# One ring of split weights, weight sums by accumulating transfers, and one more pair by seven in the second half's down projection

## The chip, the cores and the metric

The kernel runs on one core of a Trainium2 chip. The metric is device time in microseconds of one execution. Three executions of the kernel before took 1452.99 to 1454.95 us, median 1453.46 us.

## The reference

One encoder layer for 256 tokens of width 2048, all in float32. The matrix products are nearly all of the work:

- `proj = rms_norm(x) @ w_in`, 10240 columns: queries, keys and values of two attentions (windowed with grouped queries, and dilated in three patterns), and two gates of 2048 columns each;
- `merged = sigmoid(ga) * (ya @ w_branch_a) + sigmoid(gb) * (yb @ w_branch_b)`, then `x + merged @ w_out`;
- `x + (gelu(conv3(hf @ w_ffn_gate)) * (hf @ w_ffn_up)) @ w_ffn_down` with 5632 hidden columns;
- `x + sigmoid(rms_norm(x) @ w_ple_gate) * (p @ w_ple_proj)`, and a last rms norm.

## The kernel before

**Split numbers.** Every operand of a large product is split into a high and a low half in a fast 32-bit format: ScalarE (ACT) copies the high half (L310), VectorE (DVE) subtracts it from the original for the low half (L311). A product is then three matmuls (`thirds`, L413 to L415: high by high, high by low, low by high), or, where the weights are the stationary operand, one of 512 columns and one of 256 (L356, L363).

**Pieces and units.** The weights lie in DRAM as 258 pieces of 128 rows by 2048 columns (1 MB), in the order in which they are used. SyncE's queue (SP) loads a piece into one of three buffers `raw` (`load`, L251), two pieces ahead of the one being split. A piece is split in units (`produce`, L293), each `uh` or `vh` (high) and `ul` or `vl` (low). Units sit in two rings: "u" with six slots and "v" with two, each slot 1024 columns wide whatever the unit's width. `pump` (L318) splits further units whenever a slot is given back (`drop`, L330), strictly in the list's order.

**Stages.** In order of time: A (38 projection jobs, with the attention between them), four gate stages B0 to B3, each followed by the two branch products `ba` and `bb`, two halves of the output projection D0 and D1, then the MLP in two halves of 22 hidden chunks: E0 (gate and up, 44 jobs of 16 matmul pairs), F00 and F01 (down, half of the output columns each), E1, F10 and F11. At the end stand the `ple` stages pp0, pp1, G0, G2, G3.

**Seven products for eight.** B, D, F and G0 work on a pair of 128-row weight chunks by two blocks of 512 output columns at a time, a 2 x 2 x 2 block product for two halves of the tokens. A piece marked "s" does its eight products plainly. One marked "Z" or "S" does seven (M1 to M7) with sums of weight blocks and sums of activations, and adds the results at the end of the stage. A string has a letter for each piece; the second half's down projection, for instance, is "ZsZsZsZsZss", five of eleven by seven, in each of F10 and F11. Each M has a bank of the accumulator memory: M1 to M7 in seven banks, P22 in the eighth; the plain pieces use M2, M3, M4 and P22. The last piece of each string is plain. While it runs, `row_sums` (L910) adds M1, M6, M7 and M5 into the result tiles (L917 to L921), and then each of M2, M3, M4 and P22 is added when its last product is done (in D and F by `finish` of `residual`, L1033 and L1035). A seven-product piece has four units; M1 needs the first, M2 and M3 the second, M7 and M6 (M5 in an "S") the third, the other two the fourth. They run in the order M1, M7, M6 or M5, M5 or M6, M4, M2, M3, and give their units back in the order first, third, fourth, second.

**Sums of weights.** The sums of the four blocks in `raw` are made by DVE: L283 and L284 for Z (512 and 1024 columns), L289 to L291 for S (1024, 512 and 512). One sum of three blocks of a Z piece is made ahead: `sum_ahead` (L263) loads half of the three blocks into SBUF by GpSimd's queue (POOL, L269), DVE adds them (L272, L273), and POOL stores the result to DRAM (L276), from where `load` takes it in place of the first block. In A this is done for the Z pieces of B1 to D1 (tile `hb`), in E0 and E1 for those of F and G0 (tile `ahead`), at slots given by job and step (`at` and `run_due`, L596 to L605).

**Order.** The program gives an order and a priority; a planner may put instructions of one engine otherwise where their operands come late in its own estimate, save those under `keep`. On each engine the instructions then run in that fixed order, and each waits for what it needs.

## Time and profile before

| | us |
|---|---|
| median of three runs | 1453.46 |
| the profiled execution | 1453.29 |
| its span (first to last instruction) | 1451.5 |
| PE busy | 1439.8 |
| DVE busy | 1255.9 |
| ACT busy | 836.3 |
| POOL busy | 126.7 |

What lies between an execution's time and its span is the start and the end of the program. "PE" is TensorE's matmuls and "PEld" its weight loads, which overlap them. In a row of instructions stand the start, the duration, the engine, the line, the operation, the tiles written and read, their shapes and the count; in square brackets the idle time before it, and what ended it. Groups give their count, busy time and mean duration in ns, then the idle time before them. The DMA rows give the queue, the count, the size and the median time from issue to landing.

### The profile page before, as it was taken

What the parts mean: (1) busy time and instruction counts of PE and PEld (TensorE: products, weight loads), DVE (VectorE), ACT (ScalarE), POOL (GpSimd) and SP (SyncE); (2) the same over time, 40 slices, a digit from 0 to 9 for tenths busy, and PEclk for the clock granted to TensorE, in tenths of its full rate; (3) what the DMA queues carried; (4) which work ended last, traced back from release to release, by engine and by line L of the source; (5) the groups of instructions that cost most, each with busy time, mean ns of one, the idle gap of its engine ahead of it and who ended that gap; (6) DMA issues with size and microseconds to landing.
All of it is one profiled execution on the core that took longest, in us unless ns stands there. A gap on an engine that the chain in (4) does not pass through costs nothing.

```text
span 1451.5 us, 20060 instructions
## 1 busy us (share of the span) xinstructions
PE 1439.8 (99%) x7455; PEld 1231.0 (85%) x7455; DVE 1255.9 (87%) x1827; ACT 836.3 (58%) x1160; POOL 126.7 (9%) x193
## 2 busy tenths in 40 slices
PE   9999999999999999999999999999999999999997
PEld 8888888888888888788888888888888888888885
DVE  8778776779999999989787899997878799898994
ACT  7455544546656656666555566565545466564863
POOL 0112222210000000000222000000222200000000
PEclk9999999999999999999999999999999999999999
DMA  9776677764456466475777655566777765556462
GB/s 334 274 286 240 227 259 261 255 223 174 177 207 227 172 228 235 170 262 216 272 253 256 240 208 189 198 251 220 256 278 254 276 239 200 198 187 243 163 232 87
DMA packets 67805, 331.17 MB, mean 228 GB/s; under 512 B 8628, under 2 KB 13620, under 8 KB 41340
## 3 DMA queue, kind: packets, MB, share of 16 engines
q1 hardware_dynamic: 52268, 280.46, 53.7%
q0 software_dynamic: 14720, 48.25, 9.2%
q8 instruction: 58, 0.95, 0.3%
q10 hardware_dynamic: 720, 1.19, 0.2%
q14 instruction: 39, 0.32, 0.1%
HBM read 315.67 MB, written 14.20 MB: 227 GB/s over the span
## 4 chain that ended last, share of the span: by engine, by line
PE 92%; DVE 3%; issue 2%; DMA 1%; ACT 0%; POOL 0%; POOLq 0%; SPq 0%; DVEq 0%; ACTq 0%
PE bank L356 28%; PE bank L363 15%; PE bank L413 13%; PE bank L414 13%; PE bank L415 13%; PE bank L340 2%; PE bank L402 1%; PE bank L404 1%; PE bank L403 1%; PE bank L341 1%; DVE ul L311 1%; PE bank L966 1%; DMA raw<-in_wts 1%; DVE vl L311 1%; DMA xr<-in_xrow 0%
## 5 line engine op out<-in xcount | busy, mean ns | idle before, releaser
L310 ACT ACTIVATE uh<-raw 128x1024 fp32r<-128x1024 f32 (+2 forms) x519 | 515.4, 1007 | 293.1 <-PE bank L415 88.8
L311 DVE TENSOR_TENSOR ul<-raw,uh 128x1024 fp32r<-128x1024 f32 (+2 forms) x519 | 590.7, 1157 | 63.5 <-ACT uh L310 42.6
L356 PE MATMUL bank<-hf,uh 128*128 128x512 f32 x1408 | 336.6, 391 | 0.0
L356 PEld LDWEIGHTS bank<-hf,uh 128*128 128x128 f32 x1408 | 258.8, 188 | 50.6 <-DVE hf L522 0.4
L363 PEld LDWEIGHTS bank<-hf,ul 128*128 128x128 f32 x1408 | 180.7, 191 | 7.0
L363 PE MATMUL bank<-hf,ul 128*128 128x256 f32 x1408 | 183.3, 283 | 0.0
L310 ACT ACTIVATE vh<-raw 128x1024 fp32r<-128x1024 f32 x106 | 111.0, 1055 | 56.1 <-DVE raw L283 29.9
L311 DVE TENSOR_TENSOR vl<-raw,vh 128x1024 fp32r<-128x1024 f32 x106 | 127.3, 1217 | 1.7 <-ACT vh L310 0.5
L356 PE MATMUL bank<-hs,uh 128*128 128x512 f32 x432 | 103.6, 392 | 0.0
L356 PEld LDWEIGHTS bank<-hs,uh 128*128 128x128 f32 x432 | 79.5, 188 | 15.6
L414 PE MATMUL bank<-ul,act 128*128 128x512 f32 x218 | 84.8, 389 | 0.0
L415 PE MATMUL bank<-uh,act 128*128 128x512 f32 x218 | 84.8, 389 | 0.0
L413 PE MATMUL bank<-uh,act 128*128 128x512 f32 x218 | 84.5, 389 | 0.0
L505 ACT ACTIVATE t<-bank 128x256 f32<-128x256 f32 x122 | 45.4, 375 | 60.8 <-PE bank L363 50.1
L269 POOL DMA_DIRECT2D ahead<-in_wts x52 | 38.8, 747 | 378.5 <-DMA ahead<-ahead 209.3
L1112 ACT ACTIVATE gw<-gw,cl 128x256 f32<-128x256 f32 x44 | 24.1, 594 | 71.5 <-DVE gw L1109 71.4
L413 PE MATMUL bank<-uh,hs 128*128 128x512 f32 x154 | 60.8, 395 | 0.0
L272 DVE TENSOR_TENSOR ahead<-ahead 128x256 f32<-128x256 f32 x52 | 21.9, 422 | 44.7 <-DMA ahead<-in_wts 44.6
L415 PE MATMUL bank<-uh,hs 128*128 128x512 f32 x154 | 60.1, 390 | 0.0
L414 PE MATMUL bank<-ul,hs 128*128 128x512 f32 x154 | 60.0, 389 | 0.0
L363 PE MATMUL bank<-hs,ul 128*128 128x256 f32 x432 | 56.6, 284 | 0.0
L284 DVE TENSOR_TENSOR raw<-raw 128x1024 f32<-128x1024 f32 x46 | 56.0, 1217 | 0.3
(270 smaller groups left out, 2526.1 us busy)
## 6 DMA issues: line engine op xcount, KB each, us to landing
raw<-in_wts SPq DMA_DIRECT2D x205, 1024.0 KB, 4.9
raw<-in_wts SPq DMA_DIRECT2D x46, 768.0 KB, 4.6
ahead<-in_wts POOLq DMA_DIRECT2D x52, 384.0 KB, 5.1
hb<-in_wts POOLq DMA_DIRECT2D x40, 384.0 KB, 5.0
raw<-ahead SPq DMA_DIRECT2D x46, 256.0 KB, 4.9
ahead<-ahead POOLq DMA_DIRECT2D x52, 128.0 KB, 4.5
raw<-in_wts SPq DMA_DIRECT2D x12, 512.0 KB, 6.7
ahead<-hb POOLq DMA_DIRECT2D x40, 128.0 KB, 3.1
```

Source lines behind the costliest of these rows:

```text
L269: keep(nc.gpsimd.dma_start(q, wts[p][:, :3 * WIDE].rearrange("p (q c) -> p q c", c=WIDE)[:, :, cols]))
L284: nc.vector.tensor_tensor(raw[:, 2 * WIDE:], raw[:, 2 * WIDE:], view(q[0], 0, (0, 2), (1, WIDE)), op=ALU.subtract)
L310: nc.scalar.activation(hi, src, AF.Copy)
L311: nc.vector.tensor_tensor(lo, src, hi.bitcast(F32), op=ALU.subtract)
L340: nc.tensor.matmul(acc, hi[:, w], m, start=first, stop=False, skip_group_check=True)
L356: nc.tensor.matmul(acc, weights(u)[0][:, o * P:(o + 1) * P], m, start=first, stop=False, skip_group_check=True)
L363: nc.tensor.matmul(acc[:, T:], weights(u)[1][:, o * P:(o + 1) * P], m[:, :T], start=False, stop=last, skip_group_check=True)
L413: nc.tensor.matmul(acc, sh, wh, start=first, stop=False)
L414: nc.tensor.matmul(acc, sh, wl, start=False, stop=False)
L415: nc.tensor.matmul(acc, sl, wh, start=False, stop=last)
L505: keep(nc.scalar.activation(t, acc[:, T:], AF.Copy, scale=scale))
L1112: nc.scalar.activation(c[:, i], g[:, i], AF.Identity, scale=tap(1, f), bias=tap(3, f))
```

## The change

- All split weights share one store: 48 blocks of 128 columns from the start, and 16 more when the attention's memory is given back (in B0). A unit takes as many blocks as it is wide, from the front of a list of free blocks (`take`), and gives them back at its end. Where its blocks aren't neighbours, it is split in two parts, each with its own copy and subtraction.
- The seven products run in the units' order: M1, M2, M3, M7, M6, M5, M4. Signs in the sums change to fit (`sums_of`, `row_sums`, `sums_of_weights`).
- The "S" pieces are gone. Their seven places are "Z" now, so their sums are made ahead too. B0 has two of them.
- `sum_ahead` is three transfers on POOL's queue from DRAM to DRAM, a copy and two that accumulate; DVE takes no part. `spread_sums` puts the three steps of each piece two slots apart and the pieces evenly over the slots: those of B0 to B3 over the jobs of A after the eighth, those of D0 and D1 over the pieces of B1 to B3, those of F and G0 over the jobs of E0 and E1 from the thirteenth on.
- The second half's down projection has six of eleven pieces by seven in place of five, in F10 and in F11.

```diff
-GATES = ("sssssSSs", "ZsZZsSZs", "ZsZSsSZs", "ZsZSsSZs")
+GATES = ("sssssZZs", "ZsZZsZZs", "ZsZZsZZs", "ZsZZsZZs")
-DOWN = ("ZZsZsZsZsZs", "ZsZsZsZsZss")
+DOWN = ("ZZsZsZsZsZs", "ZsZZsZsZsZs")
...
-RINGS = {"u": 6, "v": 2}
+STORE = {"w": 48, "v": 16}
...
+    def take(u, n):
+        taken[u] = [free.popleft() for _ in range(n)]
+        runs = []
+        for o, (which, b) in enumerate(taken[u]):
+            if runs and runs[-1][0] == which and runs[-1][1] + runs[-1][3] == b:
+                runs[-1][3] += 1
+            else:
+                runs.append([which, b, o, 1])
+        return runs
...
-    def sum_ahead(p, h, tag):
...
-        keep(nc.gpsimd.dma_start(q, wts[p][:, :3 * WIDE].rearrange("p (q c) -> p q c", c=WIDE)[:, :, cols]))
-        def add():
-            keep(nc.vector.tensor_tensor(q[:, 0], q[:, 2], q[:, 0], op=ALU.subtract))
-            keep(nc.vector.tensor_tensor(q[:, 0], q[:, 0], q[:, 1], op=ALU.add))
-        def store():
-            keep(nc.gpsimd.dma_start(ahead[p][:, cols], q[:, 0]))
+    def sum_ahead(p):
+        ahead[p] = dram.tile([P, WIDE], F32, name="ahead%d" % p)
+        def step(n):
+            keep(nc.gpsimd.dma_start(ahead[p], wts[p][:, n * WIDE:(n + 1) * WIDE], accum_op=ALU.add if n else ALU.bypass))
+        return [partial(step, n) for n in range(3)]
...
     def sums_of_weights(raw):
-        nc.vector.tensor_tensor(q[1], q[0], q[1], op=ALU.subtract)
-        nc.vector.tensor_tensor(raw[:, 2 * WIDE:], raw[:, 2 * WIDE:], view(q[0], 0, (0, 2), (1, WIDE)), op=ALU.subtract)
+        nc.vector.tensor_tensor(raw[:, WIDE:3 * WIDE], view(q[0], 0, (0, 2), (1, WIDE)), raw[:, WIDE:3 * WIDE], op=ALU.subtract)
+        nc.vector.tensor_tensor(q[3], q[0], q[3], op=ALU.add)
...
+        made[u] = take(u, (b - a) // P)
+        for _, _, o, n in made[u]:
+            hi, lo = part_of(made[u], o, n)
+            src = raw[:, a + o * P:a + (o + n) * P]
+            nc.scalar.activation(hi, src, AF.Copy)
+            nc.vector.tensor_tensor(lo, src, hi.bitcast(F32), op=ALU.subtract)
...
-                    todo = (("M1", m1, 0, 0, 0), ("M7", sums[2], 2, 1, None), ("M6", sums[1], 2, 0, 2),
-                            ("M5", sums[0], 3, 0, None), ("M4", m4, 3, 1, 3),
-                            ("M2", m2, 1, 1, None), ("M3", sums[3], 1, 0, 1))
+                todo = (("M1", m1, 0, 0, 0), ("M2", m2, 1, 1, None), ("M3", sums[3], 1, 0, 1),
+                        ("M7", sums[2], 2, 1, None), ("M6", sums[1], 2, 0, 2),
+                        ("M5", sums[0], 3, 0, None), ("M4", m4, 3, 1, 3))
...
+    def spread_sums(pieces, slots):
+        last = len(slots) - 5
+        for e, p in enumerate(pieces):
+            first = e * last // max(len(pieces) - 1, 1)
+            for n, step in enumerate(sum_ahead(p)):
+                at(slots[first + 2 * n], step)
...
+    slots = [(i, k) for i in range(FIRST + 1, NA)
+             for k in (range(0, KC, KC // len(_JOBS[i][1])) if _JOBS[i][0] == "v" else (0,))]
+    spread_sums(summed("B0", "B1", "B2", "B3"), slots[:-3])
+    spread_sums(summed("D0", "D1"), [("B%d" % j, i, 0) for j in range(1, 4) for i in range(8)])
...
+        spread_sums(summed("F10", "F11", "G0") if half else summed("F00", "F01"),
+                    [(stage, i, 0) for i in range(12, len(jobs) - joint)])
```

More of the change, by code (lines that the diff above doesn't have):

```diff
@@ L1 @@
 import math
+from collections import deque
 from contextlib import ExitStack
+from functools import partial
 import numpy as np
@@ L247, in _encoder, with extend, part_of @@
     raws, made = {}, {}
-    state = {"raw": 0, "unit": 0, "at": 0, "early": True,
-             "u": RINGS["u"], "v": RINGS["v"]}
+    state = {"raw": 0, "unit": 0, "at": 0, "early": True}
+    store, free, taken = {}, deque(), {}
+    def extend(which, pool):
+        store[which] = [pool.tile([P, STORE[which] * P], FR, name=which + half) for half in ("h", "l")]
+        free.extend((which, b) for b in range(STORE[which]))
+    extend("w", wpool)
+    def take(u, n):
[7 more added lines that the diff above has]
+        return runs
+    def part_of(runs, o, n):
+        which, b, first, size = next(r for r in runs if r[2] <= o < r[2] + r[3])
+        assert o + n <= first + size
+        a = (b + o - first) * P
+        return [t[:, a:a + n * P] for t in store[which]]
     def load(r, a=0, b=PIECE):
@@ L337, in block @@
         u, o = _FBLOCKS[state["at"]]
-        hi, lo = weights(u)
-        w = slice(o * P, (o + 1) * P)
-        nc.tensor.matmul(acc, hi[:, w], m, start=first, stop=False, skip_group_check=True)
-        nc.tensor.matmul(acc[:, T:], lo[:, w], m[:, :T], start=False, stop=last, skip_group_check=True)
+        hi, lo = weights(u, o)
+        nc.tensor.matmul(acc, hi, m, start=first, stop=False, skip_group_check=True)
+        nc.tensor.matmul(acc[:, T:], lo, m[:, :T], start=False, stop=last, skip_group_check=True)
         state["at"] += 1
@@ L442, in cut @@
         def cut(u, i):
-            return [w[:, i * WIDE:(i + 1) * WIDE] for w in weights(u)]
+            return weights(u, 4 * i, 4)
         for i, p in enumerate(pieces):
@@ L683, in _encoder @@
     nc.sync.dma_start(hold, rows)
-    hb = big.tile([P, 2 * D * 2], F32, name="hb", tag="R1")
-    spare = [view(hb, QH * AW + BH * BW + e * 3 * T, (T, 3), (1, T)) for e in range(2)]
+    hb = big.tile([P, QH * AW + BH * BW], F32, name="hb", tag="R1")
     hba = hb[:, :QH * AW].rearrange("p (h c) -> p h c", c=AW)
@@ L857, in after, with summed @@
             attend(i, [(QH + g * HG + j, KVH + g * HG + j) for g in range(NG)], QH + j)
-    todo = [(p, h) for stage in ("B1", "B2", "B3", "D0", "D1") for p in _STAGES[stage] if _PIECES[p][0] == "Z"
-            for h in range(2)]
-    slots = [(FIRST, SUB)]
-    for i in range(FIRST + 1, NA + 2):
-        slots += [(i, k) for k in (range(0, KC, 16 // len(_JOBS[i][1])) if i < NA and _JOBS[i][0] == "v" else (0,))]
-    assert len(todo) < len(slots), (len(todo), len(slots))
-    def asked(e):
-        add, store = sum_ahead(*todo[e], spare[e % 2])
-        i, k = slots[e + 1]
-        late = k + (2 if i < NA and _JOBS[i][0] == "v" else SUB)
-        at((i, late), add)
-        at((i, late + 1), store)
-    for e in range(len(todo)):
-        at(slots[e], asked, e)
+    def summed(*stages):
+        return [p for stage in stages for p in _STAGES[stage] if _PIECES[p][0] == "Z"]
+    slots = [(i, k) for i in range(FIRST + 1, NA)
+             for k in (range(0, KC, KC // len(_JOBS[i][1])) if _JOBS[i][0] == "v" else (0,))]
+    spread_sums(summed("B0", "B1", "B2", "B3"), slots[:-3])
+    spread_sums(summed("D0", "D1"), [("B%d" % j, i, 0) for j in range(1, 4) for i in range(8)])
     for i, job in enumerate(_JOBS):
@@ L904, in open_tok @@
         held["tok"] = ctx.enter_context(tc.tile_pool(name="tok", bufs=1))
+        extend("v", held["tok"])
     def outputs():
@@ L1162, in split_last @@
             nc.vector.tensor_tensor(pl_[k], held["pr"][:, k], ph_[k].bitcast(F32), op=ALU.subtract)
-    def sevens(half):
-        stages = ["F%d%d" % (half, j) for j in range(2)] + ["G0"] * half
-        return [p for stage in stages for p in _STAGES[stage] if _PIECES[p][0] == "Z"]
     for half in range(2):
@@ L1178, in _encoder @@
         turns["e"] = 0
-        todo = [(p, h) for p in sevens(half) for h in range(2)]
+        spread_sums(summed("F10", "F11", "G0") if half else summed("F00", "F01"),
+                    [(stage, i, 0) for i in range(12, len(jobs) - joint)])
         for i, (kind, n) in enumerate(jobs[joint:]):
-            if i > 1 and todo and (i % 2 == 0 or i < LASTS):
-                held["job"] = todo.pop(0), ("act2", "S4")[i % 2]
-                one_ahead(stage)
-            finish_ahead(stage)
+            run_due(stage, i, 0)
             mlp(kind, n, product(stage, lambda k: hf[:, k, :], KC, "e"))
-        assert not todo
-        drain_ahead()
         if half:
```

86 lines of the change are left out of this document (15 added, 71 removed).

## The prediction

> **What bounds the kernel now.** I read the first part of the page, then the stages in the view that cuts the span into stretches (us, then busy time and instructions of PE, PEld, DVE, ACT, POOL, then granted clock, DMA share, GB/s). The stretches shown are the projections of A, the last gate stage B3, the output stage's second half D1, the second MLP half E1, and its down stages F10 and F11.
>
> ```profile
> span 1451.5 us, 20060 instructions
> PE 1439.8 (99%) x7455; PEld 1231.0 (85%) x7455; DVE 1255.9 (87%) x1827; ACT 836.3 (58%) x1160; POOL 126.7 (9%) x193
> ...
> 4.40:304.30 299.90, 299.55 (x1723) 262.79 (x1722) 231.81 (x397) 166.37 (x264) 53.52 (x80) 1.00 0.76 270
> 482.30:523.60 41.30, 41.30 (x186) 33.72 (x185) 41.30 (x51) 25.81 (x30) 0.00 (x0) 1.00 0.60 221
> 581.80:624.80 43.00, 42.67 (x193) 34.11 (x192) 42.90 (x54) 27.30 (x36) 0.00 (x0) 1.00 0.53 189
> 984.20:1229.00 244.80, 244.80 (x1409) 216.34 (x1408) 204.93 (x332) 137.71 (x201) 37.01 (x56) 1.00 0.69 247
> 1229.00:1285.50 56.50, 56.50 (x252) 46.83 (x251) 51.34 (x58) 31.43 (x36) 0.00 (x0) 1.00 0.55 205
> 1285.50:1343.00 57.50, 57.50 (x259) 47.50 (x258) 51.17 (x59) 33.84 (x41) 0.00 (x0) 1.00 0.59 217
> ```
>
> TensorE is busy in every stretch at a granted clock of 1.00. VectorE fills B3 and D1 as fully (41.30 of 41.30, 42.90 of 43.00), so there both engines just keep pace. A busy PE need not run at its peak, so I looked at start times. The timeline of PE, start and duration of each matmul, in F10:
>
> ```profile
> 1249.77 0.39 PE L414 MATMUL bank<-ul,act 128*128 128x512 f32 x1
> ...
> 1255.89 0.39 PE L414 MATMUL bank<-ul,act 128*128 128x512 f32 x1
> ```
>
> Between these two stand 26 others, so 27 steps take 6.12 us: **0.227 us for each matmul of 512 columns**, whatever its listed duration. Time lost is what a stage takes beyond that step. The same view has the first matmul of D1, its neighbours and the first one after it:
>
> ```profile
> 581.21 0.39 PE L413 MATMUL bank<-uh,merged 128*128 128x512 f32 x1
> ...
> 582.58 0.50 PE L413 MATMUL bank<-vh,S 128*128 128x512 f32 x1 [0.30 <-DVE c L919]
> ...
> 583.84 0.39 PE L413 MATMUL bank<-uh,merged 128*128 128x512 f32 x1
> ...
> 584.75 0.39 PE L413 MATMUL bank<-vh,S 128*128 128x512 f32 x1
> ...
> 624.74 1.52 PE L356 MATMUL bank<-hf,uh 128*128 128x512 f32 x6
> L966 PE MATMUL bank<-ident,xr 128*128 128x128 f32 x64 | 9.8, 273 | 0.0
> ```
>
> D1 has five pieces by seven and three by eight: (5 x 7 + 3 x 8) x 3 = 177 matmuls, 40.2 us, and 16 transposes at 9.8/64 = 0.15 us, 2.4 us. It took 43.5 us, so some **0.95 us is lost**, half of it in the second product, whose bank DVE's L919 emptied late. One more loss, from A, where the five matmuls ought to end at 111.77 + 5 x 0.227 = 112.91:
>
> ```profile
> 111.77 1.29 PE L356 MATMUL bank<-hs,uh 128*128 128x512 f32 x5
> 113.41 0.39 PE L711 MATMUL bank<-near,v 128*128 128x256 f32 x1 [0.35 <-DVE near L770]
> 108.93 0.42 DVE L272 TENSOR_TENSOR hb<-hb 128x256 f32<-128x256 f32 x1 [0.51 <-DMA hb<-in_wts]
> ```
>
> Attention waits 0.50 us for L770. Shortly before, DVE stood 0.51 us at an addition for a sum ahead until its load came, with everything behind it in its queue.
>
> **The change part by part.** (1) *One more pair by seven in F10 and in F11.* Each drops one of eight products: 2 x 3 matmuls x 0.227 = **-1.36 us**, on the bound engine. In exchange DVE makes 3584 columns of low halves for that piece where it made 2048, and sums over 1536:
>
> ```profile
> L311 DVE TENSOR_TENSOR vl<-raw,vh 128x1024 fp32r<-128x1024 f32 x106 | 127.3, 1217 | 1.7 <-ACT vh L310 0.5
> L284 DVE TENSOR_TENSOR raw<-raw 128x1024 f32<-128x1024 f32 x46 | 56.0, 1217 | 0.3
> L272 DVE TENSOR_TENSOR ahead<-ahead 128x256 f32<-128x256 f32 x52 | 21.9, 422 | 44.7 <-DMA ahead<-in_wts 44.6
> L291 DVE TENSOR_TENSOR raw<-raw 128x512 f32<-128x512 f32 x7 | 4.8, 681 | 0.0
> ```
>
> That is 1.22 + 0.68 of low halves and 1.22 + 0.68 of sums, 3.8 us a stage: F10 goes to 55.1 of 55.8 us, F11 to 55.0 of 56.8. B3 shows that DVE can be full without holding PE. ACT's share of it (about 1.7 us) lies inside F10's 31.43 of 56.5. The new pair's own sums of activations, about 1.5 us of DVE, fall into E1 (204.93 of 244.80). Without that cover it would be PE's wait.
>
> (2) *Sums ahead by transfers alone.* Two additions of this form (L272, L273) go for each half piece, 52 times in the E stages and 40 times in A: 2 x 0.42 x 92 = 77 us of DVE off a path that DVE doesn't set, in A and the two E stages. What PE gets of it is the wait in A: bound 0 to -0.50 us, and since the transfers that DVE waited for are no longer DVE's, I take **-0.50**. In exchange POOL issues 55 x 3 = 165 transfers of 256 KB, one copy and two accumulates a piece, where it issued 184 before. No accumulate stands in the trace. Behind a POOL wait only more of these and the few root instructions are queued; the roots come in E0 and at the end, outside the stretches in which transfers are due. The steps of one sum lie two slots apart, two jobs of 244.8/44 = 5.57 us in A and E, two pieces of about 5 us in B. If an accumulate lands in under 10 us nothing waits. The nearest row is the plain one of that size:
>
> ```profile
> raw<-ahead SPq DMA_DIRECT2D x46, 256.0 KB, 4.9
> ahead<-hb POOLq DMA_DIRECT2D x40, 128.0 KB, 3.1
> q1 hardware_dynamic: 52268, 280.46, 53.7%
> q0 software_dynamic: 14720, 48.25, 9.2%
> ```
>
> At two or three passes instead of one, 4.9 us stays below 10 or little above it, and a late sum is needed only stages later. I take 0; the other end is the first rival. Loads by SP that need a sum (55 after, 46 before) are due whole stages after their last accumulate, so the queue behind them doesn't wait.
>
> (3) *S pieces become Z.* Seven pieces lose 0.68 us of DVE each (L291): 1.2 us in B0, 3.4 in B1 to B3, a stretch where DVE has none to spare.
>
> (4) *One ring.* 64 blocks in order of use, where six and two slots of eight blocks stood; a unit of four blocks no longer takes a slot of eight, and the one used last of a Z piece is no longer held through the piece. Walking the list of units through the new free list, some 87 units fall across an end of the storage and are split in two. Each costs DVE 2 x 0.68 - 1.22 = 0.14 us and as much on ACT; about 20 lie in B1 to D1 (2.8 us at most, less since neighbours overlap), 44 in E0 and E1 under DVE's slack there. With (3) DVE enters D1 a little earlier and with more in store. Of D1's 0.95 us I take **-0.80** (bounds: 0, if DVE is no earlier; -2, if the start of E0 gains too).
>
> (5) *Products in the ring's order.* M2 and M3 move from sixth and seventh to second and third. Their banks must be emptied by then; where no other stage lies between (D1, F01, F11), the same DVE does it after its sums. The timeline around F01's start, PE's second product first, then DVE's emptying of M2 and, as the first of a pair, M3, there and at D1's start:
>
> ```profile
> 928.90 0.40 PE L413 MATMUL bank<-vh,S 128*128 128x512 f32 x1
> 928.60 0.67 DVE L1033 TENSOR_TENSOR xr<-xr,bank 128x512 f32<-128x512 f32 x1
> 930.39 1.27 DVE L1033 TENSOR_TENSOR xr<-xr,bank 128x512 f32<-128x512 f32 x2
> 582.44 0.68 DVE L1033 TENSOR_TENSOR xr<-xr,bank 128x512 f32<-128x512 f32 x1
> 584.23 1.27 DVE L1033 TENSOR_TENSOR xr<-xr,bank 128x512 f32<-128x512 f32 x2
> ```
>
> With DVE as it is, M2 would wait from 928.90 to 929.27 and M3, 0.68 later, from 929.95 to 931.02: 1.4 us. D1 alike: to 583.12, then 583.80 to 584.87, 2.3 us, 1.8 beyond the present 0.46. F11 now ends in "Zs" as well, 1.4. F10's M3 shares its bank with E1's last product; taken like M3 in F01, 1.1. Upper end 5.7 us. The lower end is 0, for the order is not rigid: in D1 the plain product on uh at 583.84 is M2, listed sixth, and it ran ahead of M5 (584.75), whose bank was late. The planner fills such holes with a product whose bank is free, and M7's is emptied first. I take **+0.6**, near the lower end.
>
> Sum: -1.36 - 0.50 - 0.80 + 0.60 = -2.06 us. The profiled execution took 1453.29 us (1.8 around its span), the median 0.17 more: 1451.2 to 1451.4, forecast **1451.3**.
>
> **The rivals.** *Accumulates crowd the loads (slower).* E1 needs 44 pieces of 1.05 MB in 244.8 us, 188 GB/s; 247 GB/s at a share of 0.69 make 358 at full share. 48 transfers (16 sums) fall due in 32 jobs, 178 us: room for (358 - 188) x 178 us = 30.2 MB, 115 passes of 0.262 MB. If a copy is two passes and an accumulate three, 128 are asked, 13 too many, 9.5 us; half of that would delay loads, and the store covers it:
>
> ```profile
> 1217.63 1.84 DVE L311 TENSOR_TENSOR ul<-raw,uh 128x512 fp32r<-128x512 f32 x2
> 1229.11 0.40 PE L413 MATMUL bank<-uh,ends 128*128 128x512 f32 x1
> ```
>
> The first low half for F10 starts 11.5 us ahead of its product, so about 10.5 us may be lost unseen. At four passes 160 are asked, 45 too many, 33 us, half 16.5: PE waits 6 us, **1457.3**. It decides from about 3.5 passes. For it: an accumulate reads twice and writes once. Against: both kinds of queue move 360 GB/s of their own time (48.25 MB in 9.2% of the span, 280.46 in 53.7%), and late sums hurt nobody by themselves. The Trainium skill, "DMA: Bandwidth & Descriptors", section Specifications, speaks against the change here: it limits one core's HBM traffic to about 358 GB/s, and by that rule the source read, the read back and the write all count. The trace agrees on the figure (358 above) but has no transfer with both ends in HBM; by the rule alone the 9.5 us of the three-pass case follow, and my sum stays.
>
> *The listed order holds on PE.* Then (5) costs 5.7, and the rest of D1's loss stays: -1.36 - 0.50 + 5.7 = +3.8, **1457.3**. For it: DVE's rows at 928 and 582. Against: the reordering at 583.84.
>
> *DVE's relief reaches further.* (5) costs nothing, all of D1's loss and a further us at E0's start go: -1.36 - 0.50 - 2.0 = -3.9, **1449.6**. For it: DVE is full up to there and gets 4.6 us in B. Against: the splits take half back.
>
> *Only the six matmuls count*, stalls merely move: **1452.1**.
>
> **How the numbers follow.** Forecast (1450.3 to 1452) 0.36, relief 0.33, only matmuls 0.13, listed order 0.08, crowded loads 0.10. A difference of 0.2% (2.9 us) is about what can be told from no change here, so faster means under 1450.5: the relief and a sixth of the forecast, 0.39. Slower means over 1456.4: both slow rivals for the most part, 0.15. The rest, 0.46, is no change. The range, 1447.8 to 1457.4, leaves out the lower tail of the relief and the upper half of the two slow cases; the likeliest one's own is 1450.3 to 1452.
>
> **What would show it.** PE with six fewer matmuls and the same 0.227 us step; DVE about 75 us less busy, in A, E0 and E1, near full in F10; no L272 or L273; no wait on L770 at 113 us; D1's second product without its hole. Wrong, if accumulates land later than 10 us and ACT waits for raw in E1 (then the first rival), or if PE shows holes at the second or third product of D1, F01, F10 or F11.

## The result: slower by 0.57%, in three places

The changed kernel took **1461.86 us** (1461.44 to 1463.62, four runs) where the kernel before took 1453.70 on the same chip (1452.99 to 1454.95, four runs): a ratio of 1.0057, 95% interval 1.004 to 1.0075. The forecast was 1451.3, the range ended at 1457.4: it was wrong, and on the side that had 0.15.

From the page of the changed kernel: span, busy times, the queue of the sums' transfers, and these transfers with their median time to landing.

```profile
span 1459.7 us, 19872 instructions
...
PE 1442.4 (99%) x7449; PEld 1231.0 (84%) x7449; DVE 1208.9 (83%) x1737; ACT 850.1 (58%) x1253; POOL 126.6 (9%) x174
...
q0 software_dynamic: 20240, 43.26, 16.8%
...
ahead<-in_wts POOLq DMA_DIRECT2D x165, 256.0 KB, 7.9
```

What the change says it does, it does: six matmuls fewer (7455 to 7449), 165 transfers, 90 instructions and 47 us less of DVE. The time went elsewhere. The stretches of A, D1, E0, E1, F10 and F11 in the view by windows (us, then busy time and instructions of PE, PEld, DVE, ACT, POOL, granted clock, DMA share, GB/s):

```profile
4.40:304.30 299.90, 299.88 (x1723) 263.33 (x1722) 206.86 (x320) 165.32 (x264) 55.98 (x76) 1.00 0.91 264
580.86:629.39 48.53, 45.50 (x194) 35.18 (x193) 43.84 (x57) 27.97 (x42) 0.00 (x0) 0.96 0.50 187
629.39:878.62 249.23, 247.97 (x1428) 218.57 (x1427) 199.29 (x323) 149.25 (x238) 55.43 (x76) 1.00 0.91 263
990.72:1235.65 244.93, 244.93 (x1409) 216.47 (x1408) 192.79 (x308) 142.37 (x222) 0.00 (x0) 1.00 0.52 186
1235.65:1291.69 56.04, 56.04 (x249) 46.10 (x247) 51.67 (x60) 33.22 (x42) 0.00 (x0) 1.00 0.57 214
1291.69:1349.26 57.57, 57.34 (x255) 46.76 (x254) 54.00 (x66) 35.25 (x47) 0.00 (x0) 1.00 0.55 204
```

D1 has no gain: it took 48.5 us where it took 43.5, PE idle for 3 of them and its clock at 0.96. DVE, the engine that was to relieve it, is busy for 43.8 of the 48.5.

The transfers did not run where they were due. E1, for whose jobs 48 of them were listed, has none (POOL 0.00, a share of 0.52 where it was 0.69); A and E0 have a share of 0.91 (0.76 and 0.69 before). On POOL's queue they wait for one another and for nothing else:

```profile
POOL ahead L291 <- DMA ahead<-in_wts: 416.5, 80, 10.6
```

So the queue runs ahead of the jobs at which the steps are listed: 75 of the 165 start in A, 6 in B, 75 in E0 and 9 in F00. Without the additions A ends 0.07 us earlier (B0's first matmul starts at 304.31, before at 304.38), and E1 is as long as before.

The table has the length of each stage in the profiled execution, from its first matmul to the next stage's first, out of the timeline of PE ("tail" is what follows F11). All of these kernels reach D1 at 580 to 583 us, so a row's differences to the first add up to that of the spans within 2 us.

| kernel | D1 | E0 | F00 | F01 | E1 | F10 | F11 | tail |
|---|---|---|---|---|---|---|---|---|
| before | 43.5 | 247.5 | 56.0 | 56.0 | 244.9 | 56.5 | 57.5 | 108.4 |
| **after** | **48.5** | **249.2** | 56.1 | 56.0 | 244.9 | 56.0 | 57.6 | **110.4** |
| e2 old rings | 44.4 | 247.5 | 58.5 | 62.0 | 245.0 | 56.0 | 57.5 | 111.8 |
| e3 order alone | 43.0 | 249.1 | 56.0 | 55.9 | 244.9 | 57.0 | 57.6 | 108.5 |
| e4 sixth pair alone | 43.3 | 247.7 | 56.1 | 56.0 | 245.9 | 63.4 | 57.4 | 109.8 |
| e6 sums alone | 45.7 | 247.5 | 60.1 | 59.8 | 244.9 | 56.5 | 57.9 | 108.7 |
| e9 s1 last | 43.3 | 250.9 | 55.9 | 56.7 | 245.0 | 56.0 | 57.8 | 110.2 |
| e11 ends in ss | 43.7 | 251.1 | 56.0 | 56.1 | 245.0 | 56.0 | 56.9 | 108.4 |
| e13 additions first | 43.0 | 251.2 | 56.0 | 57.2 | 244.9 | 56.0 | 56.9 | 108.3 |
| e18 behind three | 43.8 | 247.8 | 55.9 | 56.0 | 244.9 | 56.0 | 56.9 | 108.3 |

So the 8.2 us are D1 (+5.0), E0 (+1.8) and the tail (+2.0), less 0.4 in F10 and the small change ahead of D1. The timeline of PE in D1 (start, duration, instruction, and in brackets the wait):

```profile
603.68 0.50 PE L412 MATMUL bank<-wl,S 128*128 128x512 f32 x1 [0.72 <-DVE wl L314]
604.02 0.40 PE L413 MATMUL bank<-wh,S 128*128 128x512 f32 x1
604.25 0.60 PE L927 MATMUL bank<-ident,xr 128*128 128x128 f32 x4
606.36 0.73 PE L411 MATMUL bank<-wh,S 128*128 128x512 f32 x2 [1.51 <-ACT wh L313]
607.62 0.50 PE L412 MATMUL bank<-wl,S 128*128 128x512 f32 x1 [0.53 <-DVE wl L314]
...
609.80 0.63 PE L412 MATMUL bank<-vl,merged 128*128 128x512 f32 x1
610.23 0.63 PE L413 MATMUL bank<-vh,merged 128*128 128x512 f32 x1
610.66 0.63 PE L411 MATMUL bank<-vh,merged 128*128 128x512 f32 x1
```

Three waits for split weights, and then something new: matmuls that start 0.43 us apart where the step was 0.227. The same stretch by windows has the reason, a granted clock of 0.51:

```profile
608.00:611.50 3.50, 3.50 (x10) 2.41 (x9) 1.09 (x2) 0.60 (x1) 0.00 (x0) 0.51 0.45 149
```

And the timeline of ACT there, with the last turn-back's end on DVE below it:

```profile
604.89 0.47 ACT L514 ACTIVATE hf<-bank,cl 128x256 fp32r<-128x256 f32 x1 [1.89 <-PE bank L927]
605.26 1.99 ACT L313 ACTIVATE wh<-raw 128x1024 fp32r<-128x1024 f32 x2
607.15 0.46 ACT L514 ACTIVATE hf<-bank,cl 128x256 fp32r<-128x256 f32 x1
610.90 1.65 ACT L313 ACTIVATE vh<-raw 128x1024 fp32r<-128x1024 f32 x2 [3.28 <-PE bank L413]
...
608.62 0.48 DVE L515 SCALAR_TENSOR_TENSOR hf<-bank,cl,hf 128x256 fp32r<-128x256 f32 x1
```

A "turn-back" is four transposes on PE (L927) of finished rows of D0 into bank P22, from where ACT and DVE write them to `hf` (L514, L515). D1 has four, one after the other through that bank, from 588 to 609 us. The row at 610.90 is the clue: a split that had waited 3.28 us for PE to be done with the blocks that it overwrites.

### The profile page after: what moved, and what is told of

Same layout as the page of the kernel before. It is cut to its first block, busy times and chain, and to the rows that moved or that the text cites. A ratio compares the mean times of both kernels' runs of the same rounds, so it can differ in the third digit from the quotient of the medians.

```text
span 1459.7 us, 19872 instructions
## 1 busy us (share of the span) xinstructions
PE 1442.4 (99%) x7449; PEld 1231.0 (84%) x7449; DVE 1208.9 (83%) x1737; ACT 850.1 (58%) x1253; POOL 126.6 (9%) x174
## 3 DMA queue, kind: packets, MB, share of 16 engines
q0 software_dynamic: 20240, 43.26, 16.8%
## 4 chain that ended last, share of the span: by engine, by line
PE 94%; DVE 3%; ACT 1%; DMA 1%; issue 1%; POOLq 0%; POOL 0%; DVEq 0%; ACTq 0%
PE bank L354 28%; PE bank L361 15%; PE bank L412 13%; PE bank L411 13%; PE bank L413 13%; PE bank L338 2%; PE bank L400 2%; PE bank L402 2%; PE bank L401 2%; DVE wl L314 1%; PE bank L339 1%; ACT wh L313 1%; DMA raw<-in_wts 1%; PE bank L734 0%; PE bank L927 0%
## 5 line engine op out<-in xcount | busy, mean ns | idle before, releaser
L313 ACT ACTIVATE wh<-raw 128x1024 fp32r<-128x1024 f32 (+2 forms) x543 | 500.6, 946 | 333.5 <-PE bank L354 126.0
L314 DVE TENSOR_TENSOR wl<-raw,wh 128x1024 fp32r<-128x1024 f32 (+2 forms) x543 | 574.2, 1085 | 139.9 <-issue 61.1
L354 PE MATMUL bank<-hf,wh 128*128 128x512 f32 x1056 | 256.1, 391 | 0.0
L354 PEld LDWEIGHTS bank<-hf,wh 128*128 128x128 f32 x1056 | 194.1, 188 | 37.6
L313 ACT ACTIVATE vh<-raw 128x512 fp32r<-128x512 f32 (+1 forms) x173 | 135.7, 807 | 64.8 <-PE bank L354 21.1
L314 DVE TENSOR_TENSOR vl<-raw,vh 128x512 fp32r<-128x512 f32 (+1 forms) x173 | 154.7, 916 | 16.5 <-ACT wh L313 8.5
L361 PEld LDWEIGHTS bank<-hf,wl 128*128 128x128 f32 x1056 | 137.2, 191 | 5.2
L361 PE MATMUL bank<-hf,wl 128*128 128x256 f32 x1056 | 140.8, 283 | 0.0
L354 PE MATMUL bank<-hs,wh 128*128 128x512 f32 x432 | 103.6, 392 | 0.0
L411 PE MATMUL bank<-wh,act 128*128 128x512 f32 x209 | 81.3, 391 | 0.2 <-ACT wh L313 0.2
L413 PE MATMUL bank<-wh,act 128*128 128x512 f32 x209 | 81.3, 389 | 0.0
L361 PE MATMUL bank<-hs,wl 128*128 128x256 f32 x432 | 56.6, 284 | 0.0
```

The costliest lines, as they stand in the source:

```text
L313: nc.scalar.activation(hi, src, AF.Copy)
L314: nc.vector.tensor_tensor(lo, src, hi.bitcast(F32), op=ALU.subtract)
L354: nc.tensor.matmul(acc, weights(u, o)[0], m, start=first, stop=False, skip_group_check=True)
L361: nc.tensor.matmul(acc[:, T:], weights(u, o)[1], m[:, :T], start=False, stop=last, skip_group_check=True)
L411: nc.tensor.matmul(acc, sh, wh, start=first, stop=False)
L413: nc.tensor.matmul(acc, sl, wh, start=False, stop=last)
```

## Experiments

Three theories stood first: the product order (P), the ring with its split units (R), the sums by transfers (S). Ratios are to runs of the kernel before on the same chip, taken together with the run. The kernel before took 1453.7 to 1455.5 us on them.

### One part undone, one part alone

```diff
 e1_old_order: the changed kernel, products as before
-                todo = (("M1", ...), ("M2", ...), ("M3", ...), ("M7", ...), ("M6", ...), ("M5", ...), ("M4", ...))
+                todo = (("M1", ...), ("M7", ...), ("M6", ...), ("M5", ...), ("M4", ...), ("M2", ...), ("M3", ...))
```

> The changed kernel with the products of a piece by seven in the order of before (M1, M7, M6, M5, M4, M2, M3); ring, sums and pieces as changed. Theory P (the order makes D1 lose time: PE stands for banks and units there, then runs at half clock): about 1455, the 6 us of D1 come back. Theory R (the ring and its split units make DVE and ACT late in D1): stays at 1461 to 1463. Theory S (the sums by transfers do it): stays at 1461 to 1463.

**1466.61 us, 1.0079 (1.0052 to 1.0107).** Not what P expects, nor R or S: D1 takes 45.1 us, but E0 253.0 and F01 60.3. It is a poor test: with the units given back in another order than they were taken, the free blocks scatter. The groups by line show 781 + 236 = 1017 low halves where the changed kernel has 543 + 173 = 716, so some 300 more units are split.

```diff
 e2_old_rings: the changed kernel, two rings of whole slots
-STORE = {"w": 48, "v": 16}
+RINGS = {"u": 6, "v": 2}
...
-        made[u] = take(u, (b - a) // P)
+        hi = pool.tile([P, b - a], FR, name=ring + "h", bufs=RINGS[ring])
```

> The changed kernel with the two rings of before (six and two slots of 1024 columns); order, sums and pieces as changed. Theory R: about 1455. Theory P: stays near 1462. Theory S: stays near 1462.

**1464.18 us, 1.0043 (1.0024 to 1.0062).** The time is nearer to what P and S expect (near 1462) than to R's 1455. But D1 takes 44.4 us and E0 247.5, so these two losses come with the ring, and F00, F01 and the tail lose more than D1 and E0 got back. The waits of PE between 920 and 1000 us:

```profile
PE bank L389 <- DVE xr L971: 2.2, 2, 2.0
PE bank L332 <- DVE xr L971: 1.6, 1, 1.6
PE bank L390 <- DVE vl L290: 1.1, 1, 1.1
```

```diff
 e3_order_alone: the kernel before, Z products in the new order
-                    todo = (("M1", ...), ("M7", ...), ("M6", ...), ("M5", ...), ("M4", ...), ("M2", ...), ("M3", ...))
+                    todo = (("M1", ...), ("M2", ...), ("M3", ...), ("M7", ...), ("M6", ...), ("M5", ...), ("M4", ...))
```

> The kernel before with only the order M1, M2, M3, M7, M6, M5, M4 in its Z pieces. Theory P: 1458 to 1460, with the stall and the half clock in D1. Theories R and S: 1453 to 1455.

**1456.53 us, 1.0005 (0.9993 to 1.0017).** The time lies between the two expectations. D1 takes 43.0 us at a full clock and F01 55.9: in the two rings the order costs D1 nothing. That it isn't the order with the one ring either, e9 shows below.

```diff
 e4_down_alone: the kernel before, six pairs by seven
-DOWN = ("ZZsZsZsZsZs", "ZsZsZsZsZss")
+DOWN = ("ZZsZsZsZsZs", "ZsZZsZsZsZs")
```

> The kernel before with only the sixth pair by seven in F10 and F11. The prediction's term: six matmuls of 0.227 us fewer, 1452.1 to 1452.5. Rival: the stalls that the changed kernel shows at F11's start and in pp0 (about 0.7 and 2.1 us more than before) come from this pair: 1454 to 1455.

**1463.10 us, 1.0059 (1.0038 to 1.0079).** The part that seemed safest costs as much alone as the whole change, 6.9 us of it in F10. Its start, on PE, ACT and DVE in turn:

```profile
1236.73 0.47 PE L413 MATMUL bank<-uh,ends 128*128 128x512 f32 x1 [2.46 <-ACT uh L310]
...
1239.60 0.77 PE L413 MATMUL bank<-uh,S 128*128 128x512 f32 x1 [1.95 <-DVE pair L509]
...
1234.00 0.62 ACT L1145 ACTIVATE act<-pair 128x128 fp32r<-128x128 f32 x2 [2.74 <-DVE pair L1130]
1234.52 1.04 ACT L310 ACTIVATE uh<-raw 128x1024 fp32r<-128x1024 f32 x1
...
1236.08 0.63 ACT L310 ACTIVATE uh<-raw 128x512 fp32r<-128x512 f32 x1 [0.25 <-DMA raw<-in_wts]
...
1233.28 0.69 DVE L1130 TENSOR_TENSOR pair<-pair,gw 128x512 f32<-128x512 f32 x1
```

DVE has no idle time from 1222.4 to 1246 us and makes low halves ahead of L1130; ACT stands 2.74 us at an activation that needs L1130, with two splits behind it in its queue; PE waits for the second, which starts at 1236.08 after 0.25 us more for its load. The stage's average (51 of 56 us) said nothing of this start. Half the clock follows here too, from 1238.46 on for 6.8 us.

```diff
 e5_no_sixth: the changed kernel, five pairs by seven
-DOWN = ("ZZsZsZsZsZs", "ZsZZsZsZsZs")
+DOWN = ("ZZsZsZsZsZs", "ZsZsZsZsZss")
```

> The changed kernel with the sixth pair of the second half's down stage back by eight. Theory order (the lost time comes from the fixed order in which a planner laid out the instructions of a stage's start, and in D1 that order is due to the ring): D1 is laid out as in the changed kernel and keeps its 49.6 us; six matmuls come back (+1.36 us); 1460 to 1464. Rival price (each part has a price of its own, and the sixth pair's is the 8.2 us that it cost alone): 1461.9 - 8.2 = 1453.7, D1 43 to 44 us.

**1459.80 us, 1.0033 (1.0021 to 1.0046).** D1 takes 49.2 us, so its loss isn't the pair's. The tail goes from 110.4 to 108.2 and F10 from 56.0 to 56.7: the string with six pairs costs its 2 us in the tail (by the place of the pairs, as e11 shows below), and not in F10, where DVE has been spared E1's additions. The two parts aren't independent.

```diff
 e6_sums_alone, e12_copies_only: sums by transfers and S into Z; rings, order and down stage as before
-STORE = {"w": 48, "v": 16}
+RINGS = {"u": 6, "v": 2}
...
-DOWN = ("ZZsZsZsZsZs", "ZsZZsZsZsZs")
+DOWN = ("ZZsZsZsZsZs", "ZsZsZsZsZss")
```

> The kernel before with only the sums by transfers and S turned into Z: old rings of six and two slots, old order of products, old down stage. Theory order: the transfers cost nothing by themselves, 0.5 us is gained in A, and any loss is a standstill of PE of 1 to 3 us at the start of a stage in which PE, ACT and DVE wait for one another, with no wait for a raw load: 1452 to 1458. Rival transfers (the accumulates crowd the loads): 1457 or more, with ACT or DVE waiting for raw in E1 or B, where the share of the transfer engines is 0.8 or more.

**1465.61 us, 1.0083 (1.0056 to 1.0109).** None of the sums ahead is added on DVE any more, and it is 11 us slower: F00 and F01 lose 4 each, D1 2. The time is the rival's, at another place than it named. At F00's start ACT waited for a load of weights, used 9.7 us after SP had issued it (timeline of SP, then of ACT):

```profile
870.88 0.33 SPq L253 DMA_DIRECT2D raw<-in_wts  x1
...
880.57 0.63 ACT L289 ACTIVATE uh<-raw 128x512 fp32r<-128x512 f32 x1 [4.03 <-DMA raw<-in_wts]
```

That would be the first rival of the prediction, crowded loads. The same kernel ran once more, under the label e12_copies_only (no copies are left out):

> The kernel of e6_sums_alone once more as it is (with its accumulates), beside the others, as its 1465.6 us had the widest spread. Theory transfers at one place: its loss of 4 us at 877 to 884 us comes from a raw load that took 9.7 us to land beside accumulates, and shows again there; 1462 to 1468. Rival: it was chance of that one profile, and this profile has no wait for raw at 880 us.

**1464.45 us, 1.0061 (1.0046 to 1.0075).** F00 took 59.7 us again. The load at this place landed in 4.7 us this time, but the next one came late. From the timelines of SP, ACT and PE in turn:

```profile
881.59 0.33 SPq L256 DMA_DIRECT2D raw<-in_wts  x1
...
890.96 1.06 ACT L289 ACTIVATE uh<-raw 128x1024 fp32r<-128x1024 f32 x1 [9.39 <-DMA raw<-in_wts]
...
893.02 0.49 PE L389 MATMUL bank<-vh,act 128*128 128x512 f32 x1 [2.18 <-ACT vh L289]
```

The load is used 9.4 us after its issue. ACT stands for it with the split that PE needs behind it in its queue, and with this wait, one of 0.95 us at 894.46 for the low half, and the slower steps beside them PE loses 3.7 us, all that F00 lost. In e6 PE's waits in F00 (1.10 and 0.76 us, then half the clock) stand right behind ACT's 4.03 us as well. In the kernel before, the loads issued there at 867.82 and 880.06 us landed in 4.3 and 5.1. So with two rings S has a part in F00: transfers of sums still run there until 905 or 907 us, loads land late, and ACT's queue passes the delay on to PE. How much is due to the late load and how much to that order, no run separates; nor are the transfers separated from the S pieces made Z. F01 loses 3.8 us after the last sum has landed. In the changed kernel loads take up to 8.3 us at F00's start too, and F00 takes 56.1: its 8.2 us didn't go there.

### Which order, and what is late

e7 holds the splits of D1 in the program's order, since in the changed kernel the fourth piece's last unit stands behind the sixth's (its expectation counts the pieces from 0).

```diff
 e7_listed_d1
-            nc.scalar.activation(hi, src, AF.Copy)
-            nc.vector.tensor_tensor(lo, src, hi.bitcast(F32), op=ALU.subtract)
+            listed(nc.scalar.activation(hi, src, AF.Copy))
+            listed(nc.vector.tensor_tensor(lo, src, hi.bitcast(F32), op=ALU.subtract))
```

> The changed kernel, with the splits of D1's weights on ACT and DVE held in the order of the program; nothing else changed. Theory order: the second halves of the third piece no longer stand behind the splits of the fifth, PE's holes at 601 to 611 us and the half clock behind them go: D1 takes 43 to 44.5 us, the time is 1461.9 - 5 to 6.5 = 1455.4 to 1457. Rival throughput (87 split units cost DVE and ACT more than D1 has to spare): D1 stays at 48 us or more, 1460 or more, since the same work stands in another order.

**1467.27 us, 1.0089 (1.0072 to 1.0106)**, D1 at 50.8 us: worse. The unit had not been put late by mistake. Walking the list of units through the free list gives the reason: the fourth piece's last unit takes the eight blocks of the second piece's first half, and the fifth piece's first half takes those of its second. That second piece is plain, so two of its eight products go to bank P22, which the turn-backs hold until 608.62. Its blocks are therefore free only then. In the two rings the last unit of a Z sat in ring "v", which only such units use. Held in order, everything behind it waits as well:

```profile
604.97 0.47 PE L411 MATMUL bank<-vh,merged 128*128 128x512 f32 x1 [2.20 <-DVE hf L515]
...
606.00 1.62 ACT L313 ACTIVATE vh<-raw 128x1024 fp32r<-128x1024 f32 x2 [1.69 <-PE bank L413]
```

e9 gives these 16 blocks back one and a half to two pieces later, behind the third piece's, so that the fourth and fifth no longer get them.

```diff
 e9_s1_last (e10_s1_last_f11: the same in F11 too)
+HOLD = {('D1', 1): (3, 4)}
...
+                        if (stage, i) in HOLD:
+                            late.append((HOLD[stage, i], us[c]))
+                        else:
+                            drop(us[c])
+                    while late and late[0][0] <= (i, g):
+                        drop(late.pop(0)[1])
```

> The changed kernel; the 16 blocks of D1's second piece (by eight) go back to the ring one and a half pieces later, behind the blocks of the third piece, so that the fourth piece's last unit and the fifth piece's first no longer take them. Same work, 83 split units in place of 87. Theory block (in the one ring those two units wait for the second piece's last products, which wait for bank P22 until the fourth turn-back leaves it at some 608 us; two rings kept them apart): PE's holes at 601 to 611 us and the half clock go, D1 takes 43 to 45 us in place of 49.6, the time is 1455 to 1457. Rival dice (any new order costs some standstill at D1's start, whichever blocks the units take): D1 stays over 47 us, 1459 or more.

**1458.54 us, 1.0024 (1.0015 to 1.0033).** D1 takes 43.3 us at a full clock:

```profile
580.16:623.42 43.26, 43.10 (x195) 34.42 (x193) 41.95 (x53) 27.89 (x41) 0.00 (x0) 1.00 0.51 193
```

The same work but for four split units, the same ring and order of products, 5.3 us: the cause of D1's loss is shown. But E0 took 1.6 us back, and the total is 1.5 above what was expected.

> As the run before it, and the same in F11, the other stage that starts Z, s, Z, Z with four turn-backs through bank P22. Theory block: F11's 0.96 us lost at 1300 to 1325 us goes as well, 0.5 to 1 us under the run before it. Rival dice: F11 and the start of the projections after it lose as much as in the changed kernel (3.7 us) or more.

**1457.26 us, 1.0013 (1.0004 to 1.0022).** F11 goes from 57.8 to 56.8 us, as expected; the tail keeps its 110.4. PE waits there twice in the changed kernel:

```profile
1353.53 0.44 PE L927 MATMUL bank<-ident,xr 128*128 128x128 f32 x2 [0.64 <-DVE xr L996]
...
1363.30 0.50 PE L411 MATMUL bank<-wh,t 128*128 128x512 f32 x1 [1.05 <-ACT last L1182]
```

```diff
 e11_ends_in_ss: e10 with
-DOWN = ("ZZsZsZsZsZs", "ZsZZsZsZsZs")
+DOWN = ("ZZsZsZsZsZs", "ZsZZsZZsZss")
```

> As the run before it, with the six pairs by seven of the second half at other places, so that the down stages end in two pieces by eight as before the change (Z s Z Z s Z Z s Z s s). Theory: what the changed kernel lost at 1350 us (2.8 us against 0.7) comes from a last piece by seven but one, whose sums DVE makes late; with two pieces by eight at the end 1.5 to 2 us come back: 1452 to 1455. Rival: the place of the pairs has no effect on it, 1454.5 to 1457, with the loss at 1350 us still over 2 us.

**1455.46 us, 1.0003 (0.9994 to 1.0012).** The time is 0.5 above the theory's and within the rival's, but the tail decides: it is 108.4 us, as before the change, with six pairs still by seven.

### E0's start

What was left is E0: 251.1 us against 247.5. In the changed kernel it had lost 1.8, with one wait of PE between 620 and 660 us:

```profile
PE bank L354 <- DVE hf L515: 1.1, 1, 1.1
```

Its first eight chunks of activations come from the turn-backs in D1, the other eight from D1's own rows, which ten additions on DVE finish. In the kernel before the last of these started at 633.2 us, 8.4 after E0's first matmul; in e11 at 636.4, 12.1 after it, behind low halves for E0.

```diff
 e13_additions_first: e11, and in D1 (e14_additions_half: DEFER for ('D1', 7) alone)
+DEFER = [('D1', 6), ('D1', 7)]
...
+            listed(nc.vector.tensor_tensor(r, r, a, op=ALU.add))
...
         run_due(stage, last, 8)
+        state["listed"] = True
+        for u in held.pop("defer", []):
+            drop(u)
```

> As e11_ends_in_ss, with DVE held in this order at D1's end: the ten additions that finish D1's rows first, then the low halves of the weights that take the blocks of D1's last two pieces (44 blocks, all E0's). Same work. Theory: E0 has work for PE until its ninth chunk of activations, which waits for these rows; with the additions first the rows are 4 us earlier, the 4.4 us lost at 625 to 650 us shrink to 1 to 2, 1452 to 1453.5. Rival (E0 needs those low halves just as soon): PE waits for low halves in E0's first 15 us instead, 1455 or more.

**1455.11 us, 1.0001 (0.9992 to 1.001).** A miss: the time is the rival's, though PE doesn't wait for low halves of weights. The last addition starts at 628.4, 8 us earlier, and E0 takes 251.2 as before. The wait went on to the next link, the low halves of the turned-back chunks, which DVE made behind seven low halves of weights:

```profile
PE bank L357 <- DVE hf L530: 2.0, 2, 1.5
```

That is 0.9 us less waiting than in e11, which kept its full clock; here 3.4 us of half the clock follow from 639.4 on and take the gain back.

> As the run before it, with only the low halves of the last piece's blocks (16) held behind the additions. Theory: half the effect, the loss at 625 to 650 us 2 to 3.5 us, 1453 to 1455. Rival: PE waits for low halves, 1455 or more.

**1455.80 us, 1.0000 (0.9991 to 1.0009)**, E0 at 249.8 without the half clock. By its time a miss again.

```diff
 e17_chunks_behind_two (e18_chunks_behind_three: 3 for 2): e13, and
+        release(rest[:2])
+        if rest:
+            at(("E0", 3), release, rest[2:])
...
-        at(("E0", 2 + pair), rows_pair, which, 4 + pair, hf, 1)
+        at(("E0", min(2 + pair, 3)), rows_pair, which, 4 + pair, hf, 1)
...
+        listed(nc.vector.scalar_tensor_tensor(dst[:, T:], src, g, dst[:, :T].bitcast(F32), ...))
```

> As e13_additions_first, with DVE held at E0's start in this order: the additions of D1's rows, the low halves of two units of weights (12 blocks), the low halves of the eight turned-back chunks, then the low halves of the other 32 blocks. Same work. Theory (PE has E0's first eight chunks to do, 32 blocks, some 11 us, and then needs the chunks): the loss of 4.6 us at 625 to 650 us falls to 1 to 2 us and the half clock there goes, 1452 to 1453.5. Rival: DVE and ACT are full there and any order leaves 3 us or more, 1454.5 or more.

**1452.23 us, 0.9975 (0.9961 to 0.999).** As expected. The edit also moves the last two of E0's four turn-backs one and two jobs forward, so the gain belongs to the order of DVE and to that together.

> As the run before it, with three units (20 blocks) ahead of the chunks and 24 behind. Theory: the same within 1 us, 1452 to 1454. Rival: 1454.5 or more.

**1452.18 us, 0.9975 (0.9961 to 0.9989).** Both are faster than the kernel before (1455.51 on that chip) and than the changed one. In e18 D1 and E0 cost what they did before the change, with the ring, the transfers and the sixth pair in place:

```profile
span 1450.1 us, 19869 instructions
...
580.48:624.24 43.76, 43.00 (x195) 34.42 (x194) 41.97 (x55) 28.56 (x41) 0.00 (x0) 1.00 0.52 197
624.24:872.00 247.76, 247.67 (x1427) 218.36 (x1426) 201.57 (x325) 149.42 (x237) 55.38 (x76) 1.00 0.93 268
```

### The sixth pair

> As e13_additions_first, with five pairs by seven in the second half's down stage as before the change (Z s Z s Z s Z s Z s s). Theory: where nothing stands still the six matmuls cost what they take, 1.4 us more than e13_additions_first. Rival dice: any difference from -2 to +4 us, with a standstill in F10, F11 or the projections that shows it.

e15 is e13 with "ZsZsZsZsZss". **1456.51 us, 1.0014 (1.0004 to 1.0025)**, against 1455.11 for e13. F10 takes 56.6 us in place of 56.0 and F11 57.6 in place of 56.9, 0.68 and 0.72: in these two stages the six matmuls, no more and no less. That the medians differ by the same 1.4 us is partly luck, for the single executions of e15 spread over 5.4 us, and in the profiles D1, E0 and the tail differ by up to 1.1 us each way.

> The kernel before with only the sixth pair by seven, at the places of e11_ends_in_ss (Z s Z Z s Z Z s Z s s) in place of the change's. Theory place (the 8 us of e4_down_alone came from one activation standing in ACT's queue ahead of a split): the standstills at 1234 and 1237 us change or go, 1452 to 1458. Rival work (the pair's own 3.8 us of DVE a stage and 1.5 us in E1 are what DVE can't give): as in e4_down_alone, 1461 or more with F10's start losing over 5 us.

e16 is the kernel before with the sixth pair at e11's places. **1461.68 us, 1.0044 (1.0029 to 1.006)**, F10 at 62.5 us. Its first standstill comes at the same place as in e4 (ahead of the product at 1236.76 us, 2.45 us long). So it isn't the pair's place in the string. e2 has the old rings and the pair too, but the transfers in place of the additions, and takes 56.0 us there. It reads as if DVE could carry the pair's own work at F10's start without the additions and not with them; as e2 differs in the order of products and the S pieces too, this is argued, not shown.

### The clock

e8 prices the half clock by itself: PE is held in order in E1 of the kernel before and stands still at seven places, each a chain of round trips through ACT (it computes more than is needed, and its time says nothing else).

```diff
 e8_standstill
+                for _ in range(i // 6):
+                    b = bank("misc", P, 4)
+                    keep(nc.tensor.matmul(b, ones, c, start=True, stop=True))
+                    c = sc.tile([P, 4], F32, name="probe", bufs=1)
+                    nc.scalar.activation(c, b, AF.Copy, scale=1.0 / P)
```

> The kernel before, with PE held in the order of the program in E1 and made to stand still there on purpose at seven places 33 us apart: a chain of 0 to 6 round trips of a four-column product through ACT and back, each some 0.7 to 1.5 us. Theory gate (a standstill of PE brings half the granted clock for some 3 us soon after): standstills up to 1.5 us cost only themselves, those from 2.2 us on are followed within 4 us by 3.0 to 3.5 us of steps of 0.43 us in place of 0.227, another 1.4 to 1.7 us. Rival place (the half clock belongs to what else runs at a stage's start): no step of 0.43 us in E1 at any length. The Trainium skill, TensorE: Matmul & The Clock Gate, section What's actually happening, has the clock halved after an idle window of some 3.4 us; by that the first halving would come at a standstill of 3.4 us or more, so at the fourth place at the earliest.

The timeline of PE at the second, fourth and sixth place, the chain's first matmul and the 16 products after it, and then two stretches after the fourth by windows:

```profile
1039.01 0.28 PE L1191 MATMUL bank<-ones 128*128 128x4 f32 x2
...
1040.00 3.89 PE L357 MATMUL bank<-hf,uh 128*128 128x512 f32 x16
...
1111.64 0.28 PE L1191 MATMUL bank<-ones 128*128 128x4 f32 x2
...
1113.93 5.51 PE L357 MATMUL bank<-hf,uh 128*128 128x512 f32 x16
...
1187.60 0.28 PE L1191 MATMUL bank<-ones 128*128 128x4 f32 x2
...
1191.59 6.48 PE L357 MATMUL bank<-hf,uh 128*128 128x512 f32 x16
```

```profile
1114.00:1114.90 0.90, 0.90 (x5) 0.77 (x5) 0.00 (x0) 0.00 (x0) 0.00 (x0) 1.00 0.99 364
1115.20:1118.20 3.00, 3.00 (x9) 2.32 (x8) 1.69 (x4) 1.45 (x2) 1.32 (x2) 0.50 0.77 264
```

Sixteen products take 3.89 us after a standstill of 0.99 us, 5.51 after 2.29, 6.48 after 3.99: the theory gate holds. A standstill of 2.3 us (in which PE does only the chain's four-column products) thus costs 3.9 us; the half clock begins 1.3 us after PE resumes and lasts 3.4 us by the trace's record of the granted clock. The Trainium skill, "TensorE: Matmul & The Clock Gate", section "What's actually happening", has the clock halved after an idle window of some 3.4 us. Here 2.29 us were enough, so by this run that rule allows too much.

Where the bound lies can be read from the kept traces. In the record every stretch at half the clock before 1440 us lasts 3.413 or 6.827 us, and in e8 five of them start 37.54, 37.54, 37.55 and 40.96 us apart, 11 and 12 times 3.413. So the clock changes at the ends of equal slots of 3.41 us, wherever PE stands then. The slot that decided in D1 of the changed kernel, and the next:

```profile
604.59:608.00 3.41, 1.38 (x7) 0.66 (x6) 3.22 (x5) 2.73 (x4) 0.00 (x0) 1.00 0.00 0
608.00:611.41 3.41, 3.41 (x9) 2.38 (x8) 1.09 (x2) 0.51 (x1) 0.00 (x0) 0.50 0.41 133
```

PE is idle for 2.03 us of the first, by the waits of 1.51 and 0.53 us together. Laying such slots over all the traces (from 20 to 1440 us, the chain's products of e8 counted as idle), half the clock followed each slot with over 1.9 us idle and none with under 1.7; between them it followed some. So idle time adds up within a slot, and a bound near half of it fits; this is read from the traces, no run was made to test it.

## Why the prediction was wrong, step by step

- **(4) The ring: the step that failed.** It counted blocks (fewer wasted, DVE no later) and took -0.80 us for D1; the bounds were 0 and -2. D1 lost 5.0. The 87 split units came as counted (716 low halves for 629 units). What was left out is whose blocks a unit takes. One list in order of giving back makes a unit depend on the piece that used its blocks last, here on products that wait for a bank held by another chain of work (e7, e9). At E0's start 1.8 us more were lost, with additions and low halves that PE will need behind weights that it needs later (e13, e17).
- **No price for a standstill's echo.** Each wait was priced at its own length. D1's waits of 1.51 and 0.53 us, in one slot, were followed by 3.4 us at half the clock, some 1.6 us more (seven steps took 3.15 us in place of 1.59).
- **(1) The sixth pair.** The price of the matmuls was right: 0.68 and 0.72 us by e13 and e15. The cover was argued from averages, "DVE can be full without holding PE" and F10 at 55.1 of 55.8. At a stage's start that doesn't hold (e4, e16). It held in the changed kernel's F10, where DVE is busy for only 51.7 of 56.0, probably because of (2).
- **(5) Product order.** Right for the second and third products: nothing is lost there (F01 is 56.0 us in both, e3 can't be told from before). Its term for F11's end, "F11 now ends in "Zs" as well, 1.4", was too small even as an upper end, and the sum took 0.6 for all of (5): the tail lost 2.0, and e11, which ends in "ss", got it back.
- **(2) Sums by transfers.** No loss on PE in A, E0 or E1: right for the changed kernel, but not as argued. The steps don't lie two slots apart, and "late" had no meaning for a queue that runs ahead by itself; the transfers land in 7.9 us at the median and 11.9 at most. Of the gain of 0.50 in A the wait for L770 is gone, but B0 starts only 0.07 us earlier, as A was 0.6 behind by 78 us in this profile. DVE's saving was put at 75 us and is 47: in the kernel before, an addition listed with 0.42 us is followed 0.34 us later in the timeline, so the 184 are nearer 63 us, and the splits take some of it back.
- **The rivals.** Crowded loads held PE up nowhere in the changed kernel, though the room was reckoned for E1 and the transfers ran in E0, more densely. Loads of 1 MB landed there in 7.7 us where it was 5.0, and no wait of PE followed. Counted as the rival counts, 2 passes a copy and 3 an accumulate, E0's queues moved 46.56 + 18.82 x 8/3 = 96.7 MB in 249.2 us, 388 GB/s, an estimate and more than the 358 that it took for the limit. With the old rings the case did come, in F00 (e6, e12), so that nothing was lost here rests on more than the price of the transfers. "The listed order holds" gave 1457.3 for another reason than the true one. That a shared list of blocks could tie one piece to another's bank was nobody's case, and "stalls merely move" was given no loss. The case that ended on the slower side should have been the planner's order at the starts of stages: the changed kernel, e1, e2, e4, e5 and e6 lost 5 to 12 us, most of it there.
- **The signs of being wrong.** Neither came as put: ACT did not wait for raw in E1 at all, and the waits in D1 began 20 us behind its start, not at the second or third product. The signs covered only the rivals that were thought of.

What stays open: why the two-ring kernels with transfers (e2, e6, e12) lose in F00 and F01. In F00 of e6 and e12 it begins with a late load; in F01 and in e2 the waits say DVE's additions and splits. No run took these apart, and none had the one ring without the transfers or the S pieces made Z alone.

## What to carry to other kernels

When storage is shared between streams, ask of each user whose blocks it gets and what the last reader of those blocks waits for; the count of free blocks doesn't show it. Price a stage's start by itself, from the queue orders there, since an engine at 90% over a stage can be full for its first 15 us (e4). Ask also what holds a queue back: steps listed at a job run earlier when they wait only for one another. Where PE keeps just ahead, a standstill of 2 us can cost nearly 4, so a change that saves 1 us of matmuls has to be checked for new waits before anything else.

## What the runs showed of the hardware

- Half the granted clock (0.50) for 3.41 or 6.83 us, at the ends of equal slots of 3.41 us, after a slot in which PE was idle for more than some 1.7 to 1.9 us (D1 of the changed kernel: 2.03). In e8 a standstill of 0.99 us cost the next 16 products nothing, one of 2.29 us 1.6 and one of 3.99 us 2.6 us.
- A transfer from DRAM to DRAM that accumulates is dear for the engines. The queue of the sums moved 43.26 MB in 16.8% of the span, 176 GB/s of its own time, where its plain transfers before reached 361 (48.25 MB in 9.2%). If the 55 copies cost as much a byte as those (0.73 us each), an accumulate of 256 KB takes 1.9 us of all 16 engines, an estimate of some two and a half plain passes.
- Loads beside them got slower: a piece of 1 MB lands in 6.1 us by the page's median (4.9 before). In the changed kernel that held PE up nowhere; with the old rings a load used 9.4 us after its issue stood behind PE's wait of 2.18 us (e12).
